# Hybrid MLA/FoX decoder layer: latent columns as seven half-block products, raw operand sums kept in DRAM

## The chip, the core and the metric

One core of a Trainium2 chip runs the whole layer in one launch. The metric is the device time of that launch in microseconds (us), the median over the runs. The engines are TensorE (PE, with its weight loads PEld), VectorE (DVE), ScalarE (ACT), GpSimd (POOL) and SyncE (SP). SP and POOL issue nearly all the DMAs here, and each has its own queue (q1 for SP, q0 for POOL).

## What is computed

One decoder layer on 512 tokens of width 2048, batch 1, all float32. One input projection gives the latents and gates of eight MLA heads and the q, k, v, forget logits and gates of eight FoX heads:

```python
h = _rms_norm(x, g_pre)
proj = h @ w_in              # 768 | 512 | 64 | 1024 | 1024 | 1024 | 1024 | 8 | 1024 columns
(q_lat, kv_lat, k_rope_raw, gate_mla, fq, fk, fv, f_logit, gate_fox) = jnp.split(proj, ...)
o_mla = _mla_branch(q_lat, kv_lat, k_rope_raw, g_q, w_uq, g_kv, w_ukv, cos, sin) * silu(gate_mla)
o_fox = _fox_branch(fq, fk, fv, f_logit, b_forget) * silu(gate_fox)
o = jnp.concatenate([o_mla, o_fox], axis=-1) @ w_out
return x + _rms_norm(o, g_post)
```

In `_mla_branch` the two latents (768 and 512 columns, together the first 1280 of `w_in`) are normalised over their own width before `w_uq` and `w_ukv` are applied; both branches are causal softmax attention.

## The kernel before

**Three matmuls for one.** A float32 operand is divided into a high part rounded to the matmul format (a cast on ACT) and a low part, the rest (a subtraction on DVE). `mm3` multiplies high x high, high x low and low x high. The normalised input stands transposed in SBUF as `hh` and `hl`, 16 tiles of 128 x 512 each.

**Weights in chunks.** All weights come in one list, `chunks`, 512 KB in most cases. `chunk(i)` starts loads up to four chunks ahead on SP (`load`, tile `raw`, three buffers) and divides up to two ahead (`divide`: `whi` on ACT, `wlo` on DVE, three buffers each). A load waits on SP until the buffer's last `wlo` is done, and everything behind it in SP's order waits too.

**Order of the stages.** FoX heads in four pairs (to 408 us), the latents (408 to 525), the products of the MLA gate group "m" (525 to 605), the four pairs of MLA heads (605 to some 760, tiles `mq`, `mk`, `mv`), the output projection (from 738 on, beside the last heads). The latents go through `proj_T`: five groups of 256 columns, 16 k-tiles, two outputs of 128 x 512, so 480 matmuls of width 512 into the tiles `l`.

**Seven products.** The gate group (2048 x 1024 weights, 512 tokens) and the two halves of the output projection are multiplied in Strassen's manner. Weights and activations are each cut into 2 x 2 blocks, and seven block products `p1, p2, p4, q6, g5, g7, g3` replace eight. Each product is 8 k-tiles of four chunks, and accumulates in two PSUM banks. This needs sums of weight blocks and sums of activation blocks.

- *Weight sums* `t7, t5, t6, t4` are made in DRAM in the background, by DMA alone. The list `bg` has one entry for each sum; `add_step` works off one per step: on POOL the accumulation of the entry before (L287), on SP a copy of 512 KB from DRAM to DRAM (L290), and for the next entry a *mark* (L292), a tiny DMA whose source is the current `whi`, so that the next copy waits until PE's work has come that far. Each call of `behind` counts a k-tile in `state["tiles"]`; when the count reaches `state["pace"]`, it is set to 0 and a step is made.
- *Activation sums* `g5, q6, g3, g7` are made on DVE, divided at once into high and low parts (`operand_steps`), and for the gate group and the first two k-pairs of the output projection stored to DRAM by POOL as 512 KB of two parts (`put_away`) and fetched by SP before use (`fetch`).

**Work beside the matmuls.** `todo` holds small steps; `pump` takes some after each k-tile, `drain` all. `latent` squares a latent and multiplies it by its gain; `latent_scale` makes the normalising factor, spreads it to a row with two matmuls (`make_row`) and scales; `part_latents` divides the ten scaled latents into `qn` and `kn` during the gate products. A scheduler sets the final order on each engine, and each engine works strictly in that order.

Of the kernel before, what the change touches and what calls it, by code (L numbers as in the profile page):

```python
# [12 lines left out]
F32 = mybir.dt.float32  # L13
# [3 lines left out]
ALU = mybir.AluOpType  # L17
AX = mybir.AxisListType

P = 128  # L20
# [43 lines left out]
def tile_hybrid_layer(  # L64
# [181 lines left out]
    state = {"loaded": 0, "divided": 0, "tiles": 0, "turn": 0, "step": -1, "pace": 7}  # L246
# [29 lines left out]
    lat = [add_chunks(w_in, [(0, 256 * p, 256)], NK, 4, 256) for p in range(5)]  # L276
# [42 lines left out]
    def gate_block(j, h, c):  # L319
        k = 2 * j + 8 * h  # L320
        return w_in[0, k * P : (k + 2) * P, O_GM + 512 * c : O_GM + 512 * (c + 1)].rearrange("(k p) c -> p k c", p=P)

    sum_blocks("m", gate_block)
    add_products(
        [(n, "m") for n in ("p1", "p4", "p2", "q6", "g5", "g7", "g3")],
        lambda g, h, c: add_chunks(w_in, [(0, O_GM + 512 * c, 512)], 8, 2, 512, 8 * h),
# [134 lines left out]
    def behind(w):  # L461

        if state["step"] <= len(bg):
            state["tiles"] += 1
            if state["tiles"] >= state["pace"]:
                state["tiles"] = 0
                add_step(state["step"], w[0:1, 0, 0:16].bitcast(F32))
                state["step"] += 1
        if done:
            state["turn"] += 1  # L470
            if later and state["turn"] % 3 == 0:
                later.popleft()()
# [329 lines left out]
    def operand_steps(of, j, pair, names, raw_of, place, then=None):  # L802

        a = {}
        raw = {}

        def block(n):
            if not a:
                for h in range(2):
                    for t in range(2):  # L810
                        a[f"a{t + 1}{h + 1}"] = pair[h][:, :, t * HALF : (t + 1) * HALF]
            return raw[n] if n in raw else a[n]

        def make(n, x, y):
            raw[n] = raw_of(f"r{of}{n}{j}").rearrange("p (h c) -> p h c", h=2)
            dve.tensor_tensor(out=raw[n], in0=block(x), in1=block(y), op=ALU.subtract)

        def part(n):
            both = place(f"s{of}{n}{j}").rearrange("p x (h c) -> p x h c", h=2)
            split_into(both[:, 0], both[:, 1], block(n))  # L820
            oper.setdefault((n, of), [None] * 4)[j] = both
            if then is not None:
                then(n, of, j)

        steps = []
        for n in names:
            if n == "sums":
                steps += [
                    lambda: make("g5", "a21", "a22"),
                    lambda: make("q6", "a11", "g5"),  # L830
                    lambda: part("g5"),
                    lambda: part("q6"),
                    lambda: make("g3", "a12", "q6"),
                    lambda: part("g3"),
                    lambda: make("g7", "a21", "a11"),
                    lambda: part("g7"),
                ]
            else:
                steps.append(lambda n=n: part(n))
        return steps  # L840
# [4 lines left out]
    def head_steps(j, names, raw_of, place, then=None):  # L845

        return operand_steps("o", j, (o_of[K1[j]], o_of[K2[j]]), names, raw_of, place, then)
# [3 lines left out]
    def put_away(n, of, j):  # L851

        away[n, of, j] = dr.tile([P, 1024], F32, name=f"away{of}{n}{j}")
        pool.dma_start(
            away[n, of, j].rearrange("p (x h c) -> p x h c", x=2, h=2), oper[n, of][j].bitcast(F32)
        )

    def fetch(n, of, j):
        both = slot(f"b{of}{n}{j}", F32R)
        nc.sync.dma_start(both.bitcast(F32), away[n, of, j].rearrange("p (x c) -> p x c", x=2))  # L860
        oper[n, of][j] = both.rearrange("p x (h c) -> p x h c", h=2)
# [10 lines left out]
    def product(name, g, parts, o, first, last, rate=1, at=None, held=0, side=()):  # L872
# [5 lines left out]
        def step(j, kk, t, hi, lo):  # L878
            mm3(
                o[t], *parts(kk, t), hi[:, j, :], lo[:, j, :], first and kk == 0, last and kk == 7,  # L880
                skip_group_check=True,
            )

        rng = list(prods[name, g])
        for i in rng[: len(rng) - held]:
            hi, lo = chunk(i)
            for j in range(2):
                if at is not None and kk == at[0]:
                    at[1]()
                for t in range(2):  # L890
                    step(j, kk, t, hi, lo)
                kk += 1
                pump(rate)
                if side and not held and kk % 2 == 0:
                    side.popleft()()
# [9 lines left out]
    def x_steps(j):  # L905
# [10 lines left out]
        later.extendleft(reversed(operand_steps("m", j, pair, ("sums",), tmp, part_slot, put_away)))  # L916
# [132 lines left out]
    for j in (1, 0):  # L1049
        todo.append(  # L1050
            lambda j=j: todo.extendleft(
                reversed(head_steps(j, ("a11", "a12", "a22", "sums"), tmp, part_slot, put_away))
            )
        )
# [11 lines left out]
    raw = []  # L1066
    state["pace"] = 6
    LAT = (("q", 0, 6, QR), ("k", 6, 10, KVR))
# [4 lines left out]
    def latent(i, o, to):  # L1073

        j = int(i >= LAT[1][1])
        acc, first = accs[:, j, :], i == LAT[j][1]
        dst = acc if first else tmp(f"lq{i}")
        act.square(dst, o)
        act.mul(to, o, gcol[:, NK + i : NK + i + 1])
        if not first:  # L1080
            dve.tensor_tensor(out=acc, in0=acc, in1=dst, op=ALU.add)
        raw.append(to)

    def latent_scale(j):

        name, lo, hi, width = LAT[j]
# [14 lines left out]
        dg = diagonals(y, f"lr{name}")  # L1101

        def scale(i):
            dve.tensor_tensor(out=raw[i], in0=raw[i], in1=acc, op=ALU.mult)


        nothing = [lambda: None] * 4
        todo.extendleft(
            reversed([*nothing, *nothing[:2], lambda: make_row(acc, f"lr{name}", *dg), *nothing, *(lambda i=i: scale(i) for i in range(lo, hi))])
        )  # L1110

    for p in range(5):
        lb = [proj_bank(f"l{p}{i}") for i in range(2)]
        proj_T(lat[p], [(lb[i], P, two[i]) for i in range(2)], hh, hl)
        both = slot(f"lat{p}")
        for i in range(2):
            latent(2 * p + i, lb[i], both[:, i, :])
        if p == 2:
            wait(6)
            todo.append(lambda: latent_scale(0))  # L1120
            wait(4)
            todo.append(rotary_key)

    gm = []
    qn, kn = [], []

    def part_latents():

        for to, name, ts in ((qn, "qn", raw[:6]), (kn, "kn", raw[6:])):
            for i, t in enumerate(ts):  # L1130
                todo.append(lambda to=to, i=i, t=t, name=name: to.append(split(t, f"{name}{i}")))
# [7 lines left out]


# [27 lines left out]

    wait(8)
    todo.append(lambda: latent_scale(1))  # L1170
    A, B = ([proj_bank(f"g{n}{t}") for t in range(2)] for n in "ab")
    product("p1", "m", x_block(0, 0), A, True, True, side=fetches("q6", "m"))
    pa, pb = slot("gpa"), slot("gpb")
    scaled_copy(pa, A, 0)
    scaled_copy(pb, A, 2)
    product("p4", "m", x_block(1, 2), B, True, True, side=fetches("g5", "m")[:2])
    c21 = slot("gc21")
    scaled(c21, B, 2, pb)
    product("p2", "m", x_block(1, 0), A, False, True, side=fetches("g5", "m")[2:])
    c11 = slot("gc11")  # L1180
    scaled_copy(c11, A, 0)
    C = [proj_bank(f"gc{t}") for t in range(2)]
    product("q6", "m", operand("q6", "m"), C, True, True, side=fetches("g7", "m"))
    c12 = slot("gc12")
    scaled(c12, C, 0, pa, ALU.subtract)
    G = [proj_bank(f"gd{t}") for t in range(2)]
    product("g5", "m", operand("g5", "m"), G, True, True, side=fetches("g3", "m"))
    c22 = slot("gc22")
    scaled(c22, G, 2, pb, ALU.subtract)
    part_latents()  # L1190
# [5 lines left out]
    product("g3", "m", operand("g3", "m"), G, False, True, 2)  # L1196
# [4 lines left out]
    state["pace"] = 7  # L1201
# [3 lines left out]
    qnh, qnl = zip(*qn)  # L1205
    knh, knl = zip(*kn)


    for p in range(4):
        c = mla[p]  # L1210
        qb = [proj_bank(f"mq{p}{i}") for i in range(3)]
# [155 lines left out]
    assert state["step"] > len(bg) and not later  # L1367
# [16 lines left out]
    product("p1", 1, operand("a11", "o"), A2, True, True, side=[*fetches("q6", "o"), lambda: load_gp(0)])  # L1384
# [9 lines left out]
    product("p2", 0, operand("a12", "o"), A, False, True, 2, (6, heads_end))  # L1394
    inner.close()
# [9 lines left out]
    product("p4", 0, operand("a22", "o"), B, True, True, 2)  # L1405
# [8 lines left out]
    def three(g, C, G, f):  # L1414

        product("q6", g, operand("q6", "o"), C, True, True, side=[] if g else [*fetches("g7", "o"), lambda: load_gp(1)])
        v = og_of[0, 2 * g + 1] = slot(f"c12{g}")
        sub(v, C, p1[g])
        product("g5", g, operand("g5", "o"), G, True, True, side=[] if g else fetches("g3", "o"))
        e = og_of[1, 2 * g + 1] = slot(f"c22{g}")  # L1420
        sub(e, G, p1[g])
        product("g7", g, operand("g7", "o"), C, False, True, side=[] if g else [lambda: load_gp(2), lambda: load_gp(3)])
# [63 lines left out]
```

## Time and profile before

| | |
|---|---|
| median of 3 runs | 913.91 us (911.92 to 914.56) |
| the profiled execution | 913.89 us, its span 912.0 us |
| granted TensorE clock | 0.997 |
| busy: PE, DVE, ACT, POOL | 902.1, 597.4, 413.7, 77.1 us |
| DMA | 196.21 MB, mean 215 GB/s; q1 (SP) 152.03 MB, q0 (POOL) 43.00 MB |

The rows quoted further down come from four views. A row of a stretch has its start and end, its length, the busy time of each engine with its count of instructions, the granted clock, the DMA share and GB/s. A row of a timeline has start, length, engine, line, operation and the tiles written and read; consecutive instructions of one kind are merged and counted, and an idle time ahead of them stands in square brackets at the end. A DMA row has a queue, its packets, MB and its share of the 16 DMA engines. Matmuls are pipelined, so their lengths overlap and only the distance of their starts tells the throughput.

### The profile page before, as it was taken

To read this page: it belongs to the slowest core of one execution; us is meant where nothing else is said; L and a number is where in the kernel's file an instruction comes from. 1 tells how busy PE (TensorE), PEld (TensorE's weight loads), DVE (VectorE), ACT (ScalarE), POOL (GpSimd) and SP (SyncE) were. 2 spreads that over 40 slices of the span, in tenths; PEclk is the share of its full clock that TensorE was granted. 3 is DMA by queue.
4 is the path that set the end of the run, shared out by engine and by line. 5 is a ranking of instruction groups with operands and counts; after the bars stand their busy time and mean duration, and the time that the engine had idled before them with its cause. 6 is when DMAs were issued, how large, how long until landed. Compare 5 with 4: busy or idle time off the path is not lost.

```text
span 912.0 us, 12251 instructions
## 1 busy us (share of the span) xinstructions
PE 902.1 (99%) x4444; PEld 765.9 (84%) x4444; DVE 597.4 (66%) x1042; ACT 413.7 (45%) x771; POOL 77.1 (8%) x101
## 2 busy tenths in 40 slices
PE   8999999999999999999999999999999999999997
PEld 7988888898889988888888888888888888888885
DVE  3467779437466674673554556777978895876686
ACT  4773333234223442342434354644454465644474
POOL 1001101010111110111221100000000000000021
PEclk9999999999999999999999999999999999999999
DMA  9367876886877988887899998877322146787868
GB/s 290 92 177 188 233 192 172 220 188 182 210 218 221 259 188 229 251 242 192 253 336 310 259 319 297 301 240 179 92 84 75 47 140 223 242 319 229 276 189 254
DMA packets 119809, 196.21 MB, mean 215 GB/s; under 512 B 15650, under 2 KB 67388, under 8 KB 119748
## 3 DMA queue, kind: packets, MB, share of 16 engines
q1 hardware_dynamic: 103556, 152.03, 51.8%
q0 software_dynamic: 15456, 43.00, 22.6%
q8 instruction: 35, 0.57, 0.3%
q10 hardware_dynamic: 736, 0.40, 0.2%
q14 instruction: 26, 0.21, 0.1%
HBM read 175.45 MB, written 70.27 MB: 269 GB/s over the span
## 4 chain that ended last, share of the span: by engine, by line
PE 94%; DMA 3%; DVE 1%; ACT 1%; issue 0%; SPq 0%; ACTq 0%
PE fv L535 5%; PE l L138 4%; PE l L140 4%; PE l L139 4%; PE fg L138 3%; PE fq L140 3%; PE fq L138 3%; PE fq L139 3%; PE fg L140 3%; PE fg L139 3%; PE fk L139 3%; PE fk L140 3%; PE fk L138 3%; PE sm L578 3%; PE fv L140 2%; PE fv L138 2%
## 5 line engine op out<-in xcount | busy, mean ns | idle before, releaser
L243 DVE TENSOR_TENSOR wlo<-raw,whi 128x1024 fp32r<-128x1024 f32 (+3 forms) x193 | 228.1, 1184 | 175.5 <-ACT whi L242 168.0
L242 ACT CAST whi<-raw 128x1024 fp32r<-128x1024 f32 (+3 forms) x193 | 196.7, 1021 | 269.4 <-PE fk L139 48.7
L138 PE MATMUL l<-h,whi 128*128 128x512 f32 x160 | 63.3, 396 | 0.0
L140 PE MATMUL l<-h,wlo 128*128 128x512 f32 x160 | 62.4, 390 | 0.0
L139 PE MATMUL l<-h,whi 128*128 128x512 f32 x160 | 62.4, 390 | 0.0
L138 PE MATMUL fq<-h,whi 128*128 128x512 f32 x128 | 52.6, 411 | 0.0
L138 PE MATMUL fg<-h,whi 128*128 128x512 f32 x128 | 51.0, 398 | 0.0
L140 PE MATMUL fq<-h,wlo 128*128 128x512 f32 x128 | 50.3, 393 | 0.0
L140 PE MATMUL fg<-h,wlo 128*128 128x512 f32 x128 | 50.1, 392 | 0.0
L139 PE MATMUL fq<-h,whi 128*128 128x512 f32 x128 | 50.1, 391 | 0.0
L138 PE MATMUL fk<-h,whi 128*128 128x512 f32 x128 | 50.0, 391 | 0.0
L139 PE MATMUL fg<-h,whi 128*128 128x512 f32 x128 | 49.9, 390 | 0.0
L139 PE MATMUL fk<-h,whi 128*128 128x512 f32 x128 | 49.8, 389 | 0.0
L140 PE MATMUL fk<-h,wlo 128*128 128x512 f32 x128 | 49.8, 389 | 0.0
L140 PE MATMUL fv<-whi,h 128*128 128x256 f32 (+1 forms) x128 | 39.5, 309 | 0.0
L139 PE MATMUL fv<-wlo,h 128*128 128x256 f32 (+1 forms) x128 | 39.5, 309 | 0.0
L138 PE MATMUL fv<-whi,h 128*128 128x256 f32 (+1 forms) x128 | 39.5, 309 | 0.0
L535 PE MATMUL fv<-whi,h 128*128 128x456 f32 x128 | 39.2, 392 | 0.0
L140 PEld LDWEIGHTS l<-h,wlo 128*128 128x128 f32 x160 | 30.0, 188 | 6.4
L287 POOL DMA_DIRECT2D t<-in_w_out_dram x16 | 18.7, 1168 | 198.0 <-DMA t<-in_w_out_dram 197.6
L138 PEld LDWEIGHTS l<-h,whi 128*128 128x128 f32 x160 | 30.1, 188 | 6.0
L139 PEld LDWEIGHTS l<-h,whi 128*128 128x128 f32 x160 | 30.1, 188 | 5.7
(484 smaller groups left out, 2210.3 us busy)
## 6 DMA issues: line engine op xcount, KB each, us to landing
raw<-in_w_in_dram SPq DMA_DIRECT2D x84, 512.0 KB
t<-in_w_out_dram SPq DMA_DIRECT2D x32, 512.0 KB
raw<-t SPq DMA_DIRECT2D x32, 512.0 KB
raw<-in_w_out_dram SPq DMA_DIRECT2D x24, 512.0 KB
t<-in_w_out_dram POOLq DMA_DIRECT2D x16, 512.0 KB, 8.3
t<-t POOLq DMA_DIRECT2D x16, 512.0 KB, 8.2
awaymg<-smg POOLq DMA_DIRECT2D x12, 512.0 KB, 6.8
bmg<-awaymg SPq DMA_DIRECT2D x12, 512.0 KB
```

The lines of the kernel that those rows point to most:

```text
L138: pe.matmul(o, ah, bh, start=first, stop=False, **kw)
L139: pe.matmul(o, ah, bl, start=False, stop=False, **kw)
L140: pe.matmul(o, al, bh, start=False, stop=last, **kw)
L242: act.copy(hi[:, :m], raw[:, :m])
L243: dve.tensor_tensor(out=lo[:, :m], in0=raw[:, :m], in1=hi[:, :m].bitcast(F32), op=ALU.subtract)
L287: pool.dma_start(to.rearrange("p (k c) -> p k c", k=2), second, accum_op=ALU.add)
L535: pe.matmul(banks[t][:, :n], a[k][:, tss[t]], b[:, j, :], start=k == 0 and m == 0, stop=k == NK - 1 and m == 2,)
L578: pe.matmul(s[:, :nn], a[:, qs], c[:, :nn], start=(i == 0), stop=(i == len(pairs) - 1))
```

## The change

- The first 1024 latent columns are computed as seven products (group "l"), in turn with those of the gate group. They are `turned`: the weights are the stationary operand, so the result comes out with the latent columns on the partitions, 128 x 256 per block; the activation operands are those of the gate group and are shared. Only the last 256 columns still go through `proj_T`. `lat_sum` and `lat_less` combine the blocks.
- The sums of the latent weights join `bg` (64 entries instead of 48).
- Activation operands go to DRAM as raw fp32 sums (256 KB each) and are divided after the fetch (`part_fetched`).
- The steps of `bg` are counted in `paced`, which `product` calls too; the count is lowered by the pace. The pace is 6, then 4, then 1000 from product p1 of the latents on, 6 from product g5 of the gate group on, 2.5 in the MLA heads, 4 in the output projection.
- A latent is scaled and divided in one step (`latent_part`), ten of them in `todo` from product q6 of the gate group on.

```diff
-            if state["tiles"] >= state["pace"]:
-                state["tiles"] = 0
+            if state["tiles"] >= state["pace"]:
+                state["tiles"] -= state["pace"]
...
-    lat = [add_chunks(w_in, [(0, 256 * p, 256)], NK, 4, 256) for p in range(5)]
+    lat = add_chunks(w_in, [(0, 1024, 256)], NK, 4, 256)
...
+    for g in "lm":
+        sum_blocks(g, lambda j, h, c, g=g: in_block(g, j, h, c))
     add_products(
-        [(n, "m") for n in ("p1", "p4", "p2", "q6", "g5", "g7", "g3")],
+        [
+            *((n, g) for n in ("p1", "p2", "p4") for g in "lm"),
+            *((n, g) for g in "lm" for n in ("q6", "g5", "g7", "g3")),
+        ],
...
     def fetch(n, of, j):
         both = slot(f"b{of}{n}{j}", F32R)
-        nc.sync.dma_start(both.bitcast(F32), away[n, of, j].rearrange("p (x c) -> p x c", x=2))
-        oper[n, of][j] = both.rearrange("p x (h c) -> p x h c", h=2)
+        nc.sync.dma_start(both[:, 1, :].bitcast(F32), away[n, of, j])
+        oper.setdefault((n, of), [None] * 4)[j] = both.rearrange("p x (h c) -> p x h c", h=2)
+
+    def part_fetched(n, of, j):
+        both = oper[n, of][j]
+        split_into(both[:, 0], both[:, 1], both[:, 1].bitcast(F32))
...
+            for f in range(2):
+                c = slice((2 * t + f) * P, (2 * t + f + 1) * P)
+                mm3(
+                    o[t][:, f * HALF : (f + 1) * HALF], hi[:, j, c], lo[:, j, c], *parts(kk),
+                    first and kk == 0 and f == 0, last and kk == 7, skip_group_check=True,
+                )
...
                 pump(rate)
+                paced(hi)
...
+    def latent_part(i):
+        j = int(i >= 6)
+        dve.scalar_tensor_tensor(
+            out=raw(i), in0=raw(i), scalar=gcol[:, NK + i : NK + i + 1], in1=accs[:, j, :],
+            op0=ALU.mult, op1=ALU.mult,
         )
+        latents[i] = split(raw(i), f"ln{i}")
...
+    state["pace"] = 1000
...
+    product("q6", "l", sums_wide("q6"), C, True, True, side=along(divisions("g5", "m"), fetches("g7", "m")), turned=True)
...
+    for i in range(10):
+        todo.append(lambda i=i: latent_part(i))
...
+    state["pace"] = 6
+    product("g5", "m", operand("g5", "m"), G, True, True)
...
-    state["pace"] = 7
+    state["pace"] = 2.5
```

How the order on the engines moves, at two places. In what follows g5/0 is the first of the four chunks of the gate group's product g5, g3/1 the second of product g3.

SP, from the last chunks of product g7 to the plain chunks of product g3 (read from `w_in`), before:

```order
L221 DMA raw_5110<-t7m_107 128x1024
L860 DMA bmg_5128<-awaymg_3232 128x1024
L221 DMA raw_5130<-t7m_108 128x1024
L860 DMA bmg_5148<-awaymg_3588 128x1024
L230 DMA raw_5153<-in_w_in_dram 128x2x512
L230 DMA raw_5177<-in_w_in_dram 128x2x512
L230 DMA raw_5201<-in_w_in_dram 128x2x512
L230 DMA raw_5225<-in_w_in_dram 128x2x512
```

and at the same place now (`t_...` are sums of output weights, `whi_5365` and so on the chunk whose high half a mark waits for):

```order
L221 DMA raw_5411<-t7m_124 128x1024
L290 DMA t_152<-in_w_out_dram 128x2x512
L290 DMA t_144<-in_w_out_dram 128x2x512
L292 DMA t_148<-whi_5365 1x16
L292 DMA t_153<-whi_5365 1x16
L230 DMA raw_5446<-in_w_in_dram 128x2x512
L290 DMA t_148<-in_w_out_dram 128x2x512
L290 DMA t_153<-in_w_out_dram 128x2x512
L292 DMA t_165<-whi_5389 1x16
L292 DMA t_157<-whi_5389 1x16
L230 DMA raw_5470<-in_w_in_dram 128x2x512
L290 DMA t_165<-in_w_out_dram 128x2x512
```

Between two chunk loads there now stand two copies and two marks, where there was nothing or an operand fetch.

DVE, from a chunk of product g7 to one of product g3, before (`qn`, `kn` are low halves of latents, `wlo` those of chunks):

```order
L243 TENSOR_TENSOR wlo_5204<-raw_5153,whi_5203 128x1024
L243 TENSOR_TENSOR wlo_5228<-raw_5177,whi_5227 128x1024
L130 TENSOR_TENSOR kn_5237<-lat_4531,kn_5237 128x512
L130 TENSOR_TENSOR kn_5246<-lat_4531,kn_5246 128x512
L130 TENSOR_TENSOR kn_5264<-lat_4683,kn_5264 128x512
L243 TENSOR_TENSOR wlo_5255<-raw_5201,whi_5254 128x1024
```

and now, from the low half of chunk g7/1 to that of g7/3 (L1165 scales a latent, `ln` is its low half):

```order
L243 TENSOR_TENSOR wlo_5414<-raw_5363,whi_5413 128x1024
L130 TENSOR_TENSOR ln_5511<-lat_4344,ln_5511 128x512
L130 TENSOR_TENSOR ln_5524<-lat_4345,ln_5524 128x512
L1165 SCALAR_TENSOR_TENSOR lat_4345<-lat_4345,gcol,ls 128x512
L1165 SCALAR_TENSOR_TENSOR lat_4780<-lat_4780,gcol,ls 128x512 x2
L130 TENSOR_TENSOR ln_5543<-lat_4345,ln_5543 128x512
L130 TENSOR_TENSOR ln_5556<-lat_4780,ln_5556 128x512
L243 TENSOR_TENSOR wlo_5449<-raw_5387,whi_5448 128x1024
L130 TENSOR_TENSOR ln_5578<-lat_4780,ln_5578 128x512
L1165 SCALAR_TENSOR_TENSOR lat_4781<-lat_4781,gcol,ls 128x512 x2
L1165 SCALAR_TENSOR_TENSOR lat_3743<-lat_3743,gcol,ls 128x512
L130 TENSOR_TENSOR ln_5591<-lat_4781,ln_5591 128x512
```

Seven latent operations now stand between two chunks' low halves, where up to four stood before.

225 lines of the change are left out of this document (145 added, 80 removed).

## The prediction, made before the changed kernel ran

> **What bounds the kernel now.** I read the busy times on the page first, then the stretches of the projection stages.
>
> ```profile
> PE 902.1 (99%) x4444; PEld 765.9 (84%) x4444; DVE 597.4 (66%) x1042; ACT 413.7 (45%) x771; POOL 77.1 (8%) x101
> 410.00:526.00 116.00, 116.00 (x532) 96.15 (x531) 57.30 (x84) 44.44 (x70) 20.72 (x27) 1.00 0.96 268
> 526.00:608.00 82.00, 81.71 (x375) 67.60 (x374) 56.26 (x75) 44.31 (x59) 0.00 (x0) 1.00 0.84 288
> 608.00:740.00 132.00, 131.97 (x752) 114.74 (x751) 107.23 (x216) 66.45 (x161) 2.81 (x3) 1.00 0.39 110
> ```
>
> TensorE (PE) is the bound: 902.1 of 912.0 us, and it hardly stops in the latent stage (410 to 526), the gate products (526 to 608) or the MLA heads (608 to 740). So its time is the number of matmuls times their spacing, plus any stop that the change makes. The durations on the page overlap; the spacing is read from start times. In the timeline of PE these two rows of width 512 stand 84 matmuls apart, and the two of width 256 stand 42 apart:
>
> ```profile
> 254.92 0.39 PE L140 MATMUL fk<-h,wlo 128*128 128x512 f32 x1
> 273.96 0.39 PE L140 MATMUL fk<-h,wlo 128*128 128x512 f32 x1
> ...
> 175.88 0.28 PE L138 MATMUL fv<-whi,h 128*128 128x256 f32 x1
> 180.92 0.28 PE L138 MATMUL fv<-whi,h 128*128 128x256 f32 x1
> ```
>
> 19.04/84 = 0.2267 us at width 512, and 5.04/42 = 0.1200 us at width 256. Half the width costs 53% of the time.
>
> The third thing to see is how little room the gate products leave. Their chunk holds 12 matmuls of width 512, so PE eats one in 2.72 us. VectorE (DVE) near their end:
>
> ```profile
> 584.04 1.40 DVE L1148 SCALAR_TENSOR_TENSOR gc<-gd,hcol,gpb 128x512 f32<-128x512 f32 x2
> 585.36 1.28 DVE L130 TENSOR_TENSOR qn<-lat,qn 128x512 fp32r<-128x512 f32 x2
> 586.56 1.22 DVE L243 TENSOR_TENSOR wlo<-raw,whi 128x1024 fp32r<-128x1024 f32 x1
> 587.69 2.49 DVE L130 TENSOR_TENSOR qn<-lat,qn 128x512 fp32r<-128x512 f32 x4
> 590.10 2.35 DVE L243 TENSOR_TENSOR wlo<-raw,whi 128x1024 fp32r<-128x1024 f32 x2
> 592.37 1.89 DVE L130 TENSOR_TENSOR kn<-lat,kn 128x512 fp32r<-128x512 f32 x3
> 594.18 1.22 DVE L243 TENSOR_TENSOR wlo<-raw,whi 128x1024 fp32r<-128x1024 f32 x1
> 595.32 0.68 DVE L130 TENSOR_TENSOR kn<-lat,kn 128x512 fp32r<-128x512 f32 x1
> 595.92 1.40 DVE L1148 SCALAR_TENSOR_TENSOR gc<-gc,ncol,gc 128x512 f32<-128x512 f32 x2
> 597.24 1.40 DVE L1148 SCALAR_TENSOR_TENSOR gc<-gc,hcol,gc 128x512 f32<-128x512 f32 x2
> 598.55 1.21 DVE L243 TENSOR_TENSOR wlo<-raw,whi 128x1024 fp32r<-128x1024 f32 x1
> ```
>
> No row has an idle time behind it: DVE is full from 584 on, and PE loses only the 0.3 us of the stretch above. Back to back, a low half of a latent costs 0.62 us (2.49/4), a scaled sum 0.70, a chunk's low half 1.18.
>
> **The matmuls.** Of the 480 latent matmuls of width 512, 96 stay and 384 go; seven products of 8 k-tiles, 4 blocks and 3 terms add 672 of width 256. 384 x 0.2267 = 87.0 us less, 672 x 0.1200 = 80.6 us more: **-6.4 us**, all on the path, as nothing else on PE changes in number. This sign holds as long as a matmul of width 256 takes under 0.1295 us.
>
> The Trainium skill ("TensorE: Matmul & The Clock Gate", Back-to-back issue gap) gives N/2.4 + 2.5 ns when warm, 215.8 and 109.2 ns here, by which it would be -9.5 us. The trace does not agree (226.7 and 120.0 ns, both some 11 ns longer).
>
> **Seven products instead of proj_T: chunks.** 28 chunks of 512 KB replace 16: 12 more loads, casts and low halves. PE takes 24 x 0.1200 = 2.88 us per latent chunk and 2.72 per gate chunk. The gate products of before live on the same diet (288 GB/s, PE short by 0.3 us), with 512 KB operand fetches between; the fetches now halve. DVE gets 1.18 for the chunk, 0.62 for an operand division, and 1.4 of sums per product: 8.6 of 11.5 us. Bank reads lie behind the product of the other group that runs between. I take 0 us here; up to 3 if a fetch delays a load.
>
> **Raw sums put away, divided on return.** As many divisions as before (30 operands), later. Those of the gate group fall into the latent products (above); four fall into the first MLA heads, where DVE has 25 of 132 us free; the other ten, of 0.62 us, fall into the output products. Half the bytes go out and back. 0 us, up to 2 in the output products.
>
> **The latents' end.** Before, ten scalings ran early, and only the ten low halves stood in the full stretch. Now scaling and low half stand together, at about 0.65 + 0.62 us each, with two row copies and four scaled sums, between the low halves of chunks g7/1 and g3/0. They can't start sooner: the first row copy needs a matmul that stands 42 matmuls into product g5. Let t be counted from the start of product g5. DVE gets the rows at 11 and is through chunk g7/1 at 17, where PE wants it at 14.9. The next two chunks have 7 latent operations each ahead of them: 7 x 0.63 + 1.18 = 5.6 us against 2.72, twice 2.9 us late. Then g3/0 stands behind the scaled sums, which need the end of g7 (4 x 0.70 + 1.18, 4 us), and g3/1 behind four gate operations (3 us). Together **about 15 us**, between 12 and 17.
>
> **The block sums' debt.** Setting the pace to 1000 doesn't drop the count: `tiles` goes on rising through eleven products, to about 88, and is now lowered by the pace and no longer set to 0. At pace 6 each further call fires a step: two per chunk, 18 from g5/0 to g3/0. So SyncE (SP) gets, between two chunk loads, two DRAM copies of 512 KB and two marks, and the copies wait until the marks of the round before have landed. Four marks (L292) with what follows, in the latent stage of before, in SP's timeline:
>
> ```profile
> 423.59 0.24 SPq L292 DMA_DIRECT2D t<-whi  x1
> 424.85 0.37 SPq L230 DMA_DIRECT2D raw<-in_w_in_dram  x1
> 425.27 0.56 SPq L290 DMA_DIRECT2D t<-in_w_out_dram  x1
> ...
> 443.28 0.24 SPq L292 DMA_DIRECT2D t<-whi  x1
> 444.73 0.37 SPq L230 DMA_DIRECT2D raw<-in_w_in_dram  x1
> 448.16 0.56 SPq L290 DMA_DIRECT2D t<-in_w_out_dram  x1
> 455.80 0.24 SPq L292 DMA_DIRECT2D t<-whi  x1
> 457.06 0.37 SPq L230 DMA_DIRECT2D raw<-in_w_in_dram  x1
> 459.85 0.56 SPq L290 DMA_DIRECT2D t<-in_w_out_dram  x1
> 460.51 0.57 SPq L230 DMA_DIRECT2D raw<-in_w_in_dram  x1
> 461.29 0.34 SPq L292 DMA_DIRECT2D t<-whi  x1
> 463.10 0.37 SPq L230 DMA_DIRECT2D raw<-in_w_in_dram  x1
> 467.36 0.60 SPq L290 DMA_DIRECT2D t<-in_w_out_dram  x1
> ```
>
> A mark keeps SP for 1.26 us (455.80 to 457.06), a copy for 0.66 (459.85 to 460.51), and from mark to copy it takes 1.7, 4.9, 4.1 and 6.1 us; the 1.7 with an idle queue ahead of the mark. A round is then that wait, two copies and the first mark: wait + 2.6 us. I take 4.1 (the two longer ones shared the DMA with stores that run elsewhere now): 6.7 us. The ends are 4.3 and 8.7; I lean to the upper rows, because now two copies always stand ahead of the marks.
>
> Copies 3 and 4 issue at about t = 9, as they stand behind the load into the buffer that chunk g5/3 frees. The second chunk of query weights has its last part behind copy 17: seven rounds later, 9 + 7 x 6.7 = 56. It lands some 4.5 us on and takes 1.9 to divide: 62.4. Without stops PE would want it after three products of 10.9 us, 0.9 us of matmuls for the rows, and 18 matmuls of the first query chunk: 32.6 + 0.9 + 4.1 = 37.6. So PE is **24.8 us** late (8 to 39 for the two ends). DVE's 15 us lie inside it: both hold PE at the same chunks, and the later one counts, so that 15 is the least. Behind this chunk the debt is nearly paid and the heads have DMA to spare (0.39 of it busy before).
>
> **The sum.** The profiled execution took 913.89 us (span 912.0 plus 1.9), the median of the runs is 913.91: no correction. 913.9 - 6.4 + 24.8 = **932.3 us**.
>
> **Rivals.**
> *VectorE alone.* If rounds take under 5.3 us (waits under 2.7), the queue keeps ahead of DVE and the 15 us decide: 913.9 - 6.4 + 15 = 922.5 (919.5 to 924.5). For it: the mark that took 1.7 us, and copies that are no longer mixed with stores. Against it: no mark with a transfer fresh ahead of it took under 4.1. 20%.
>
> *The DMA engines saturate.* For it, two neighbouring stretches of 8 us, without and then with accumulations running, queue by queue, and the latent stage as a whole:
>
> ```profile
> q1 hardware_dynamic: 875, 3.20, 100.2%
> ...
> q0 software_dynamic: 397, 1.02, 83.4%
> q1 hardware_dynamic: 148, 0.45, 17.8%
> ...
> DMA packets 17345, 31.12 MB, mean 268 GB/s; under 512 B 968, under 2 KB 8648, under 8 KB 17338
> ```
>
> SP's queue (q1) moved 3.20 MB in 528:536 and 0.45 MB in 520:528, while the accumulations of POOL's queue (q0) had 83% of the engines. Up to the second query chunk stand 17 copies, 10 loads and about 15 accumulations, 42 x 0.524 = 22 MB. At 268 GB/s that is 82 us, from t = -3 to 79; with the division 81, so 43 us late: 950. Against it: an accumulation waits for its copy, so POOL can't keep its queue full. 12%. The Trainium skill ("DMA: Bandwidth & Descriptors", Queues, rings and completion order) has each engine turn between its queues packet by packet, which speaks for this case; the two stretches agree in kind.
>
> *Faster after all.* The lead hides everything: three raw buffers and chunks divided two ahead give PE about 8 us of stock, so it runs dry only where rounds stay above 2.72 us for long, and only if DVE's rows between the low halves of g7/0 and g3/0, 23 us by the durations above, fit into four chunks' 10.9. Then 913.9 - 6.4 = 907.5. DVE's own rows speak against it. 9%. A stop that just eats the 6.4 us leaves no change: 2%.
>
> **Numbers.** The forecast has 57%. I call 0.3% (2.7 us) the least that a measurement of this kernel tells from no change. Faster 0.09, same 0.02, slower 0.89. The range takes in the DVE case and the longer rounds up to 8.7 us (913.9 - 6.4 + 39 = 946.5): 918 to 947, leaving out the fast case and most of the saturated one.
>
> **What would show it.** Right: latent products at 0.120 us per matmul with PE full until product g5; PE idle of 20 to 30 us between g5 and the second query chunk; SP rounds of two L290 and two L292 some 6 to 7 us apart; casts waiting on raw. DVE full from g5's end to g3/0. Wrong: PE full through g7 and g3 (faster), or stops in the latent products themselves, or a spacing at width 256 over 0.13 us.

## The result, and the profile after

The changed kernel takes 964.89 us (median of 4 runs, 962.62 to 968.46); the kernel before took 913.03 on the same chip. The ratio is 1.057 (1.0531 to 1.061): 52 us slower, where 932.3 us, at most 947, had been forecast. The profiled execution took 962.62 us, its span 960.8.

Where the time went is read from the starts of the stages. The timeline of PE before, at the first matmul of the latents, of the gate group's product g5, of the first MLA heads and of the output projection:

```profile
408.78 0.39 PE L138 MATMUL l<-h,whi 128*128 128x512 f32 x1
...
570.20 0.39 PE L138 MATMUL gd<-whi,bmg 128*128 128x512 f32 x1
...
605.20 0.39 PE L138 MATMUL mq<-qn,whi 128*128 128x512 f32 x1
...
737.96 0.48 PE L138 MATMUL oa<-whi,boa 128*128 128x512 f32 x1
```

and the same four after:

```profile
406.22 0.39 PE L138 MATMUL l<-h,whi 128*128 128x512 f32 x1
...
560.14 0.48 PE L138 MATMUL gdm<-whi,bmg 128*128 128x512 f32 x1
...
631.54 0.39 PE L138 MATMUL mq<-ln,whi 128*128 128x512 f32 x1
...
786.18 0.48 PE L138 MATMUL oa<-whi,boa 128*128 128x512 f32 x1
```

From latents to g5 the new kernel is 7.5 us quicker (153.9 against 161.4); from g5 to the heads it loses 36.4 (71.4 against 35.0), from there to the output projection 21.9 (154.6 against 132.8), and behind it 0.6. With the 2.6 us of the start that is the 48.8 us by which the spans differ. The stretches of the kernel after (start and end, length, busy time of PE, PEld, DVE, ACT and POOL, granted clock, DMA share, GB/s):

```profile
406.00:560.00 154.00, 154.00 (x1019) 141.57 (x1017) 98.08 (x114) 76.50 (x98) 5.72 (x8) 1.00 0.76 230
...
575.00:632.00 57.00, 33.72 (x102) 23.09 (x100) 25.63 (x35) 16.89 (x22) 11.07 (x11) 0.73 1.01 246
632.00:690.00 58.00, 42.87 (x198) 34.64 (x198) 28.09 (x46) 18.83 (x37) 8.79 (x9) 0.88 1.06 259
```

PE is full from the latents to product g5, and from 575 on stands still for 23.3 and 15.1 us in two stretches in which the DMA engines are busy throughout and VectorE less than half of the time. What PE waits for between 575 and 690 us (us in total, times, longest), and what ScalarE's casts wait for there:

```profile
PE gcm L138 <- ACT whi L242: 11.3, 3, 7.4
PE mq L138 <- ACT whi L242: 8.4, 1, 8.4
PE gdm L138 <- ACT whi L242: 8.3, 2, 7.2
...
ACT whi L242 <- DMA t<-whi: 24.4, 9, 7.1
```

Of the seven casts of chunks from 575 to 625 us none waits last for its own load. Six wait for marks (`t<-whi`) and one for PE: a mark reads the high half of an earlier chunk, and there are three such buffers, so the next cast into that buffer has to wait until the mark has landed. Only from 630 on, with the query weights (`in_w_uq`), does a cast wait for a load (19.0 us in three waits). The chain of work that ended last runs through the same marks (start and time from issue to landing, in us):

```profile
576.98 5.10 DMA t<-whi
...
583.57 11.13 DMA t<-whi
...
596.17 5.06 DMA t<-whi
...
602.75 12.66 DMA t<-whi
```

SP's next copies wait for the same marks, and the loads stand in SP's order behind the copies. SP's timeline after:

```profile
565.94 1.85 SPq L290 DMA_DIRECT2D t<-in_w_out_dram  x2
...
575.71 1.22 SPq L290 DMA_DIRECT2D t<-in_w_out_dram  x2
...
582.10 1.42 SPq L290 DMA_DIRECT2D t<-in_w_out_dram  x2
...
584.70 0.40 SPq L230 DMA_DIRECT2D raw<-in_w_in_dram  x1
594.72 1.41 SPq L290 DMA_DIRECT2D t<-in_w_out_dram  x2
...
601.25 1.46 SPq L290 DMA_DIRECT2D t<-in_w_out_dram  x2
...
615.42 1.22 SPq L290 DMA_DIRECT2D t<-in_w_out_dram  x2
...
636.24 0.56 SPq L290 DMA_DIRECT2D t<-in_w_out_dram  x1
```

The rounds have the forecast's form, but between 575.71 and 615.42 four of them take 39.7 us: 9.9 us each, not 6.7, alternately short (6.4 and 6.5) and long (12.6 and 14.2). The marks take 34 of the 39.7 us, 8.5 each, where the prediction had 4.1. The queues between 590 and 610 us, with packets, MB and share of the 16 engines:

```profile
q1 hardware_dynamic: 1747, 3.36, 56.2%
q0 software_dynamic: 608, 1.67, 46.3%
```

The engines are full, and POOL's accumulations (q0) hold 46% of them for a third of the bytes. (Such a share is the time that the packets took; whether they spend it in the engines or waiting for the memory behind them, no run here separates.) Per 512 KB (0.524 MB) that is 1.75 us on q1 and 2.91 us for an accumulation. A round of two copies, a load and two accumulations then costs 3 x 1.75 + 2 x 2.91 = 11.1 us of engine time.

### The profile page after: what moved, and what is told of

Read it like the earlier page. It is cut to its first block, busy times and chain, and to the rows that moved or that the text cites. A ratio compares the mean times of both kernels' runs of the same rounds, so it can differ in the third digit from the quotient of the medians.

```text
span 960.8 us, 12945 instructions
## 1 busy us (share of the span) xinstructions
PE 912.9 (95%) x4732; PEld 781.3 (81%) x4732; DVE 619.3 (64%) x1066; ACT 424.4 (44%) x779; POOL 87.5 (9%) x105
## 4 chain that ended last, share of the span: by engine, by line
PE 84%; DMA 12%; DVE 2%; SPq 1%; ACT 1%; issue 0%; ACTq 0%; DVEq 0%
DMA t<-whi 5%; PE fv L545 4%; DMA raw<-in_w_uq_dram 4%; PE fg L138 3%; PE fq L140 3%; PE fq L138 3%; PE fq L139 3%; PE fg L140 3%; PE fg L139 3%; PE fk L139 3%; PE fk L140 3%; PE fk L138 3%; PE sm L588 2%; PE fv L140 2%; PE fv L139 2%; PE fv L138 2%
## 5 line engine op out<-in xcount | busy, mean ns | idle before, releaser
L243 DVE TENSOR_TENSOR wlo<-raw,whi 128x1024 fp32r<-128x1024 f32 (+3 forms) x205 | 242.9, 1186 | 223.8 <-ACT whi L242 213.6
L242 ACT CAST whi<-raw 128x1024 fp32r<-128x1024 f32 (+3 forms) x205 | 209.4, 1022 | 337.2 <-PE fk L139 48.5
L138 PE MATMUL mq<-ln,whi 128*128 128x512 f32 x72 | 30.6, 425 | 10.3 <-ACT whi L242 8.4
L139 PE MATMUL mq<-ln,whi 128*128 128x512 f32 x72 | 29.6, 411 | 0.0
L140 PE MATMUL mq<-ln,wlo 128*128 128x512 f32 x72 | 29.5, 413 | 0.0
L1409 POOL DMA_DIRECT2D c<-in_x_dram x8 | 7.1, 963 | 238.9 <-ACT c L1408 238.7
L605 ACT ACTIVATE pf<-sf,stf 128x128 f32<-128x128 f32 (+3 forms) x32 | 16.9, 528 | 26.9 <-DVE stf L603 26.9
L140 PEld LDWEIGHTS fq<-h,wlo 128*128 128x128 f32 x128 | 24.0, 188 | 5.4
```

What stands on the lines that cost most here:

```text
L138: pe.matmul(o, ah, bh, start=first, stop=False, **kw)
L139: pe.matmul(o, ah, bl, start=False, stop=False, **kw)
L140: pe.matmul(o, al, bh, start=False, stop=last, **kw)
L242: act.copy(hi[:, :m], raw[:, :m])
L243: dve.tensor_tensor(out=lo[:, :m], in0=raw[:, :m], in1=hi[:, :m].bitcast(F32), op=ALU.subtract)
L605: act.activation(p, s[:, :n], AF.Exp, bias=st[:, 0:1], accum_out=st[:, 1:2])
```

## Experiments

Times are compared as ratios with the kernel before, run on the same chip in turn (911.4 to 912.3 us there).

**1. The kernel after without the debt.**

```diff
     state["pace"] = 6
+    state["tiles"] = 0
     product("g5", "m", operand("g5", "m"), G, True, True)
```

> The count is set to 0 where the pace returns to 6, so the 18 overdue steps are not fired between g5/0 and g3/0; four steps fall into products g5, g7 and g3, the rest into the MLA heads. Theory debt: all of the loss that came from the steps goes (41.1 us of PE stops and 13.6 us of matmuls at a lowered clock in the profile after), and only VectorE's end is left: 913.0 - 6.4 + 15 = 921.6 us, between 918 and 926. Rival VectorE: the scaling and low halves of the latents hold PE for much more than 15 us by themselves, so the time stays above 940. Rival hidden: VectorE holds nothing once the loads come in time, 906.6 us.

Measured: 913.92 us, ratio 1.0023 (1.0008 to 1.0038). One line gives back all but some 2 us of the loss, and more than was expected of it. The stretches of its profile:

```profile
575.00:600.00 25.00, 22.37 (x107) 18.25 (x106) 23.65 (x33) 15.37 (x22) 2.38 (x3) 1.00 0.93 257
600.00:640.00 40.00, 36.60 (x188) 30.47 (x187) 27.26 (x46) 18.84 (x37) 4.78 (x6) 0.96 0.92 231
```

PE stops for 2.6 + 3.4 = 6.0 us in place of 38.4. So the debt is the cause, and VectorE's end costs far less than the 15 us put down for it. What is left are three stops of the gates (3.4, 1.6 and 1.1 us between 575 and 660 us); none waits for a chunk's low half, which is what the 15 us were counted at. VectorE's timeline in this run:

```profile
585.23 1.22 DVE L243 TENSOR_TENSOR wlo<-raw,whi 128x1024 fp32r<-128x1024 f32 x1
586.36 2.07 DVE L1165 SCALAR_TENSOR_TENSOR lat<-lat,gcol,ls 128x512 f32<-128x512 f32 x3
588.35 1.28 DVE L130 TENSOR_TENSOR ln<-lat,ln 128x512 fp32r<-128x512 f32 x2
589.55 1.22 DVE L243 TENSOR_TENSOR wlo<-raw,whi 128x1024 fp32r<-128x1024 f32 x1
```

At most five latent operations stand here between two low halves of chunks, where the order shown ahead of the prediction had seven, and the low halves stand 2.3 to 4.3 us apart, where the prediction had 5.6. In the kernel after VectorE was not even full there. It had time to wait 7 us for a late chunk:

```profile
596.06 1.23 DVE L243 TENSOR_TENSOR wlo<-raw,whi 128x1024 fp32r<-128x1024 f32 x1 [6.99 <-ACT whi L242]
```

The code of the latents is the same in both. The scheduler's order changed when the steps went.

**2. The debt without its accumulations.**

```diff
-        if n > 0:
+        if n > 0 and not state.get("bare"):
             to, _, second = bg[n - 1]
             pool.dma_start(..., accum_op=ALU.add)
...
     state["pace"] = 6
+    state["bare"] = True
```

> The overdue steps stay, but from product g5 on no accumulation is issued on POOL's queue (the later sums of output weights lack their second block). Theory bytes: a round of two copies, two accumulations and a chunk load moves 2.62 MB at 253 GB/s, 10.4 us; without the accumulations 1.57 MB, 6.2 us. By the prediction's own sum the second query chunk is then 9 + 7 x 6.2 + 6.4 - 37.6 = 21 us late instead of 50, and the lowered clock takes some 7 us: 913.0 - 6.4 + 21 + 7 = 935 us, between 925 and 945. Rival marks: the round is the time that a mark takes behind the copies in SP's own queue, and POOL's accumulations run beside it: unchanged within 1%, 955 to 966 us.

Measured: 925.93 us, ratio 1.0146 (1.0112 to 1.018), at the low end of what the theory of bytes gave, and 30 us from the rival. The accumulations on POOL's queue, whose sums PE does not need before the output projection, carry about three quarters of the loss: 5.7% falls to 1.5%. The marks still stand in SP's queue, but they land sooner: from 574.87 to 597.87 us four rounds take 23.0 us, 5.75 each, no copy waits longer than 3.8 us for a mark, and the casts wait 3.7 us for marks in all. The edit also takes away the later accumulations, in the heads, which the kernel before has too; so the burst's own part may be somewhat less.

**3. The debt without marks.**

```diff
-        if n + 1 < len(bg):
+        if n + 1 < len(bg) and not state.get("bare"):
             nc.sync.dma_start(bg[n + 1][0][0:1, 0:16], mark)
```

> The overdue steps stay with copies and accumulations, but from product g5 on no mark is issued, so no copy on SP waits for a mark to land. Theory bytes: the same 2.62 MB per round pass through the same engines, so PE waits as long: 955 to 966 us. Rival marks: a round is only the issue of two copies and a load, some 2 us, the queue keeps ahead of PE, and VectorE's 15 us decide: 922 us, up to 930.

Measured: 968.32 us, ratio 1.0614 (1.0593 to 1.0636). The number fits the theory, but the run can't speak for it: without its mark nothing ties a copy to its place, and the scheduler put the copies of the output weights at the head of the program, where PE stopped instead: SP's timeline has four of these copies in a row at 17.09 us. A stretch behind them:

```profile
20.00:160.00 140.00, 100.96 (x395) 79.97 (x394) 51.31 (x88) 45.93 (x108) 26.34 (x27) 0.85 1.05 266
```

39 us of stops at a DMA share of 1.05, in another place. The question of the marks was put again in run 4.

**4. The marks on ScalarE's queue.**

```diff
-            nc.sync.dma_start(bg[n + 1][0][0:1, 0:16], mark)
+            (act if state.get("apart") else nc.sync).dma_start(bg[n + 1][0][0:1, 0:16], mark)
...
     state["pace"] = 6
+    state["apart"] = True
```

> The debt is kept with all its copies and accumulations, in their places; only the marks from product g5 on are issued by ScalarE on its own queue, so that a mark no longer stands behind two copies of 512 KB in SP's queue. Theory bytes: the engines move the same 2.62 MB per round, so the time stays within 1%: 956 to 970 us. Rival marks: a mark with an empty queue ahead of it took 1.7 us, a round is then 4.3 us, and by the prediction's sum PE is late by no more than VectorE's part: 914 to 931 us.

Measured: 959.38 us, ratio 1.0517 (1.0492 to 1.0542). What SP's copies wait for between 575 and 690 us (total, times, longest), in the kernel after and then in this run:

```profile
SPq L290 <- DMA t<-whi: 52.0, 8, 10.7
```

```profile
SPq L290 <- DMA t<-whi: 8.3, 2, 7.0
```

SP's waits for marks are nearly gone, and yet its chunk loads (at 584.63, 594.76 and 603.23 us) keep their rhythm, 9.3 us apart. ScalarE's casts in the same stretch now wait for those loads:

```profile
ACT whi L242 <- DMA raw<-in_w_in_dram: 18.2, 3, 7.1
```

PE gains 5 us of 52. The wait for the mark was mostly the form in which SP and the casts felt full engines, not their cause: with the marks out of the way the loads themselves come late. The marks are not quite gone as a cause, since in ScalarE's own order they hold one cast back for 8.6 us, so 5 us may be a little less than they cost.

**5. Plain copies for accumulations.**

```diff
-            pool.dma_start(..., second, accum_op=ALU.add)
+            how = {} if state.get("plain") else {"accum_op": ALU.add}
+            pool.dma_start(..., second, **how)
...
     state["pace"] = 6
+    state["plain"] = True
```

> The debt is kept, with every transfer in its place and on its queue; only the accumulations from product g5 on are made plain copies of the same 512 KB (the later sums of output weights then hold the second block alone). In the profile after, between 590 and 610 us, q1 had 56.2% of the engines for 3.36 MB and q0 46.3% for 1.67 MB: 1.75 us per copied and 2.91 us per accumulated 512 KB. Theory: an accumulated byte costs the engines 1.66 times a copied one, so a round of five transfers falls from 11.1 to 8.8 us, the stops by about a fifth: 948 to 957 us. Rival: only the count of bytes matters: unchanged, 960 to 968 us.

Measured: 947.54 us, ratio 1.0381 (1.0346 to 1.0417): a third of the loss goes though every byte that the profile counts is still moved. POOL's queue between 590 and 610 us:

```profile
q0 software_dynamic: 659, 2.40, 33.1%
```

512 KB on q0 now take 33.1% x 20 / 2.40 x 0.524 = 1.45 us of the engines, half of the 2.91 of an accumulation.

**6. The debt on the kernel before.**

```diff
-    state["pace"] = 6
+    state["pace"] = 1000
...
+                if state.get("due", 0) and state["step"] <= len(bg):
+                    state["due"] -= 1
+                    add_step(state["step"], hi[0:1, 0, 0:16].bitcast(F32))
+                    state["step"] += 1
...
+    state["due"] = 18
     product("g5", "m", operand("g5", "m"), G, True, True, side=fetches("g3", "m"))
```

> The kernel before with its own latents and operands, only its steps withheld from the latent stage on and 18 of them fired from the gate group's product g5 on, one per k-tile. Theory debt: the burst by itself costs what it cost in the kernel after, about 41 us of stops and 14 us of lowered clock, less what operand fetches of 512 KB no longer compete for: 945 to 967 us. Rival: the burst hurts only together with the new end of the latents on VectorE: below 925 us.

Measured: 971.06 us, ratio 1.0644 (1.0625 to 1.0663), a little over the range. The old kernel with the old latents loses as much by the burst alone, and its casts wait 40.0 us for marks between 570 and 690 us:

```profile
570.00:640.00 70.00, 42.91 (x143) 30.54 (x142) 24.55 (x31) 18.64 (x25) 11.13 (x11) 0.78 1.02 276
```

**7. Matmuls in the stops.** The granted clock of 0.73 and 0.88 in the stretches after was no part of the prediction. Behind a stop the matmuls follow at 0.43 us instead of 0.227; PE's timeline after:

```profile
596.08 1.22 PE L138 MATMUL gcm<-whi,bmg 128*128 128x512 f32 x2 [7.36 <-ACT whi L242]
...
597.93 0.63 PE L140 MATMUL gcm<-whi,bmg 128*128 128x512 f32 x1
598.36 0.63 PE L139 MATMUL gcm<-wlo,bmg 128*128 128x512 f32 x1
```

Taken over both stretches, 33.7 us of busy time at 0.73 and 42.9 at 0.88 would lose 33.7 x 0.27 + 42.9 x 0.12 = 14 us, by estimate. Is that a loss of its own?

```diff
+    FILL = {("g7", "m", 2): 7, ("g7", "m", 4): 12, ("g7", "m", 6): 32, ("g3", "m", 2): 31, ("g3", "m", 4): 6}
+    def fill(n, hi):
+        if n:
+            to = bank("pv", "fill", 1)
+        for _ in range(n):
+            pe.matmul(to, hi[:, 0, :P], hi[:, 1, :], start=True, stop=True, skip_group_check=True)
...
+            fill(FILL.get((name, g, kk), 0), hi)
```

> The kernel after, with 7, 12, 32, 31 and 6 matmuls of width 512 more, whose results nobody reads, ahead of the five chunks of products g7 and g3 that PE waits for most: 88 x 0.2267 = 19.9 us of work laid into the stops, so that PE doesn't pause there. Theory clock: the slow matmuls behind these stops (1.5, 2.4, 1.6, 2.3 and 2.0 us in the profile after) run at full clock, and the time falls by 5 to 9 us, to 956 to 960. Rival engines: the chunks land when the DMA engines let them, and a faster matmul only waits longer for the next one: unchanged, 962 to 967 us.

Measured: 966.82 us, ratio 1.0595 (1.0573 to 1.0616), as after.

```profile
575.00:632.00 57.00, 44.75 (x174) 34.02 (x173) 22.08 (x29) 12.52 (x16) 11.07 (x11) 0.94 1.03 250
```

The clock in the products rises from 0.73 to 0.94 (the added matmuls counted in), and the products end no earlier: their last matmul starts at 631.72 us, in the kernel after at 631.31. While transfers decide when a chunk is there, a quick matmul only waits longer for the next. For the heads the run says nothing: the order there changed, and PE now stops 7.9 us for gates.

**8. Without the debt, with earlier row copies.**

```diff
     state["pace"] = 6
+    state["tiles"] = 0
...
-    wait(6)
+    wait(10)
...
-    product("q6", "m", operand("q6", "m"), C, True, True)
+    product("q6", "m", operand("q6", "m"), C, True, True, 2)
```

> No overdue steps (as in the first run of this call), and VectorE's end begins about 7 us earlier: product q6 of the gate group takes two steps of the list per k-tile, with ten empty steps in place of six ahead of the row copies. Theory: with the debt gone VectorE is the last cause, and its end now has four more k-tiles to spread over: 8 to 15 us less than the run without debt, 907 to 914 us. Rival: what is left without the debt isn't VectorE's: the same time as that run within 2 us.

Measured: 912.46 us, ratio 1.0003 (0.9991 to 1.0016), 0.2% under run 1, far less than the 8 us that VectorE's rows were thought to give. What was left were stops of the gates; the longest, 2.7 us, was the second query matmuls' wait for a scaled sum that frees their bank.

**9. GpSimd scales the latents, and no step runs in the gate products.**

```diff
-        if i >= 8:
-            act.copy(raw(i), o)
+        act.mul(raw(i), o, gcol[:, NK + i : NK + i + 1])
...
-        dve.scalar_tensor_tensor(
-            out=raw(i), in0=raw(i), scalar=gcol[:, NK + i : NK + i + 1], in1=accs[:, j, :],
-            op0=ALU.mult, op1=ALU.mult,
-        )
+        pool.tensor_tensor(out=raw(i), in0=raw(i), in1=accs[:, j, :], op=ALU.mult)
...
-    state["pace"] = 6
...
-    state["pace"] = 2.5
+    state["pace"], state["tiles"] = 2, 0
```

> No step of the block sums runs in the gate products at all (the 23 that are left run in the MLA heads, one per two k-tiles), a latent is multiplied by its gain on ScalarE when it is squared, and by its row on GpSimd (1.28 us by the only row of such an operation), so VectorE has ten operations of 0.69 us less in products g5 to g3. Theory: without the debt the last stops (6.2 us, and 2.3 us of lowered clock, at 593 to 610 us in the run without debt) are VectorE's, and go: the time before less 6.4 us, up to 2 us more, so 905 to 908 us where the kernel before takes 911.4. Rival: those stops are the gates' own chain (scaled sum, transposition, tanh, product), which only moves: 912 to 914 us.

Measured: 920.74 us, ratio 1.0096 (1.0068 to 1.0124). Both theories missed it. GpSimd's and VectorE's groups:

```profile
L1164 POOL TENSOR_TENSOR lat<-lat,ls 128x512 f32<-128x512 f32 x10 | 17.2, 1756 | 121.2 <-DVE ls L449 121.2
```

```profile
L130 DVE TENSOR_TENSOR ln<-lat,ln 128x512 fp32r<-128x512 f32 x8 | 11.6, 1497 | 0.0
...
L1213 DVE SCALAR_TENSOR_TENSOR gc<-gdm,hcol,gpb 128x512 f32<-128x512 f32 x2 | 1.4, 739 | 0.0
```

Beside GpSimd's work a low half of a latent takes 1.50 us on VectorE, against 0.68 in run 1 (mean of the group between 571 and 592 us in both). What VectorE was to be spared it lost on its own operations. The edit changes two things at once: run 12 below has the same pace of steps without GpSimd's scaling, and its ratio is 1.0036, so part of the 1.0096 is likely the steps'.

**10 to 12. Three trims of run 8.** Run 10 issues the scaled sum at once; run 11 also puts all gates behind product g3; run 12 is run 10 with no steps in the gate products (as in run 9).

```diff
-    todo.append(lambda: scaled(c12, G, 0, c12))
+    scaled(c12, G, 0, c12)
```

> As the run without debt and with early rows, and the scaled sum that frees the bank of product g3 is issued right behind the product, not put at the end of the list: it stood behind a chunk's low half, and PE waited 2.7 us at the second query matmuls for the bank. Theory: that stop goes, 909 to 911 us where the kernel before takes 911.4. Rival: the low half of the chunk is late in its place: the same as that run, 912 to 913 us.

Measured: 911.69 us, ratio 0.9985 (0.997 to 1.0), between the two. The stop of 2.7 us is gone, and one of 2.4 us for a gate stands in the first heads instead.

```diff
-    for f in range(4):
-        todo.append(lambda f=f: gate(f, c11, c21))
...
-    for f in range(4, 8):
-        todo.append(lambda f=f: gate(f, c12, c22))
+    for f in range(8):
+        todo.append(lambda f=f: gate(f, *((c11, c21) if f < 4 else (c12, c22))))
```

> As the run before it in this call, and the four gates of the upper half are put behind product g3 too, so that no transposition stands in products g7 and g3 waiting for VectorE's scaled sums (stops of 1.3 and 0.9 us). Theory: another 1 to 2 us less, 907 to 910 us. Rival: the gates then meet the first MLA heads' own work on VectorE, and PE stops there instead: 911 to 915 us.

Measured: 913.04 us, ratio 1.0001 (0.9985 to 1.0018): the rival's side.

```diff
-    state["pace"] = 6
-    state["tiles"] = 0
     product("g5", "m", operand("g5", "m"), G, True, True)
...
-    state["pace"] = 2.5
+    state["pace"], state["tiles"] = 2, 0
```

> As the second run of this call, and the four steps of the block sums in products g5 to g3 are moved into the MLA heads too (one per two k-tiles there). Theory: the chunk loads meet no accumulation in the products, 1 to 2 us less than the second run. Rival: with more steps in the heads their weight loads are late instead, as in the run in which GpSimd scaled the latents: 1 to 4 us more.

Measured: 916.26 us, ratio 1.0036 (1.0016 to 1.0056), the rival again, a little over its 1 to 4 us. With the steps away PE is full in the products (560 to 600 us; VectorE, busy for 39.7 of the 40 us, holds nothing up), and stands still for 4 us from 600 to 640 and 3 us from 640 to 737, in the heads, instead.

Run 10 is the best found; its gain of 0.15% is under the 0.3% that can be told from no change. By the starts of its stages, against the kernel before, it is 7.4 us quicker from latents to g5 (154.0), 1.6 slower in the gate products (36.6, 0.9 of it the row matmuls) and 5.1 slower in the heads (137.9 against 132.8). So the gain of the matmuls is spent mostly in the heads.

## Why the prediction was wrong, point by point

- **The matmuls, -6.4 us: right.** The 7.5 us from latents to g5 hold 0.9 us of row matmuls that now stand behind g5's start; 6.6 remain. In the timeline after, two matmuls of width 256, 28 apart:

```profile
501.53 0.28 PE L139 MATMUL gcl<-bmq,whi 128*128 128x256 f32 x1
...
504.89 0.28 PE L140 MATMUL gcl<-bmq,wlo 128*128 128x256 f32 x1
```

  3.36/28 = 0.1200 us, as taken.
- **Chunks, raw sums and divisions at nothing: right.** PE is full in all 154 us of the products with group "l", and the output projection changed by 0.6 us. The 2.6 us at the start are no effect of these: runs 1 and 8 carry the same code there and begin the latents at 405.81 and 407.76 us.
- **The place of the loss: right; its form: half right.** The debt stops PE from product g7 on; run 1 takes it away and run 6 makes it alone. But the prediction had the loads late behind the copies, with "casts waiting on raw" as its sign. In the products the casts wait for marks instead, which hold the buffers of the high halves; only at the second query chunk, where the sum was made, is it a load behind a copy.
- **The size of a round, 6.7 us: wrong, and the step that failed.** The wait from mark to copy, 4.1 us, was read off the latent stage, with one copy and one accumulation to a mark, and carried over as if it were a latency. It measured 8.5 us on the average, because it is mostly the time the DMA engines need for what is queued: a round took 9.9 us, 11.1 by engine time. The forecast's seven rounds, from copies 3 and 4 (565.94) to copy 17 (636.24), took 70.3 us in place of 46.9. With them the prediction's own path reads 5.8 + 70.3 + 9.5 = 85.6 us after the start of g5, where it had 9 + 46.9 + 6.4 = 62.3: the whole miss at this chunk is in the rounds, give or take 3 us at either end. Run 2 agrees with the rest of the sum: with its rounds of 5.75 us the sum gives 913.9 - 6.4 + (9 + 7 x 5.75 + 6.4 - 37.6) = 925.6, and 925.9 were measured (927 by the ratio); that the two agree so closely is partly luck, as the sum counts no loss behind this chunk. The argument against the saturated rival, "an accumulation waits for its copy, so POOL can't keep its queue full", fell: q0 had 45.5% of the engines over the whole 72 us from g5 to the heads:

```profile
q0 software_dynamic: 2248, 5.82, 45.5%
```

- **The saturated rival, 12%: right in kind, and at its place in size.** It had PE 43 us late at the second query chunk. PE gets there at 645.8, t = 85.6, against 37.6 without stops: 48. With 27 plain transfers at 1.75 and 15 accumulations at 2.91 its sum is 91 us of engine time where it had 82.
- **"Behind this chunk the debt is nearly paid": wrong.** Accumulations and late head weights filled the engines to 690 us, at a share of 1.06 from 632 on. PE's stop ahead of the second query chunk, 8.4 us, is part of the 21.9 us lost between heads and output projection; the rest, some 13 us, came after it, and neither forecast nor rival had it.
- **VectorE's 15 us as a floor: wrong.** Run 1 stops for 6.0 us, all of it for gates. Seven latent operations per chunk were counted in an order that the scheduler had made with the late loads in it, and were taken for a property of the code.
- **The range's top, 947,** followed from rounds of 8.7 us and left the saturated case outside. It should have reached past it, for q0's 83% of the engines in the rows of before was direct evidence.

What stays open is why run 6 loses 0.7% more than the kernel after with the same count of overdue steps, why the rounds are alternately short and long, and what exactly costs run 10 its 5 us in the heads. None was tried further.

## What to carry to other kernels

Cost background transfers in engine time per queue, and sum it over the stretch: a wait that a transfer shows in the trace may be mostly the work queued ahead of it, as here, and then won't hold when that work is doubled. A tiny transfer that reads a buffer holds the buffer until it has landed, so a mark between full queues can stop the engine that fills the buffer. A counter that goes on counting while its consumer is off becomes a burst at the moment the consumer returns; look at what a pace does on re-entry before looking at anything else. An order printed by a scheduler belongs to the whole program, and another edit can dissolve the crowding that one reads in it.

## What the runs showed of the hardware

- **An accumulating DMA costs the engines twice a plain one.** 512 KB from DRAM to DRAM on POOL's queue: 2.91 us of the 16 engines as an accumulation (kernel after), 1.45 as a copy (run 5), both with the engines nearly full. In the rows of before from 520 to 528 us it was more: 83.4% x 8 / 1.02 x 0.524 = 3.4 us.
- **Behind short stops the clock sometimes falls.** In the timeline after, pauses of 1.13 and 0.53 us, two matmuls apart, are followed by 0.43 us per matmul:

```profile
623.53 0.73 PE L138 MATMUL gdm<-whi,bmg 128*128 128x512 f32 x2 [1.13 <-ACT whi L242]
624.79 0.50 PE L139 MATMUL gdm<-wlo,bmg 128*128 128x512 f32 x1 [0.53 <-DVE wlo L243]
...
625.77 0.63 PE L140 MATMUL gdm<-whi,bmg 128*128 128x512 f32 x1
626.20 0.63 PE L138 MATMUL gdm<-whi,bmg 128*128 128x512 f32 x1
```

  Two pauses of the same form, no shorter, are not; here 0.24 us per matmul follow:

```profile
577.05 0.73 PE L138 MATMUL gcm<-whi,bmg 128*128 128x512 f32 x2 [1.41 <-ACT whi L242]
578.31 0.50 PE L139 MATMUL gcm<-wlo,bmg 128*128 128x512 f32 x1 [0.53 <-DVE wlo L243]
...
578.89 0.40 PE L139 MATMUL gcm<-wlo,bmg 128*128 128x512 f32 x1
579.13 0.40 PE L140 MATMUL gcm<-whi,bmg 128*128 128x512 f32 x1
```

  So the length of the pauses alone does not decide. The first pair came some 7 us behind a stop of 7.2 us and a run of slow matmuls, the second behind full work; whether that is the reason, no run shows. The Trainium skill ("TensorE: Matmul & The Clock Gate", HAM oscillation) warns of pauses over some 3.4 us. The trace agrees that the pace halves behind longer pauses (7.36 us in run 7's rows), and shows that shorter ones can be followed by it too.
- **GpSimd's arithmetic slows VectorE's with two SBUF inputs.** 0.68 to 1.50 us for a low half, and 1.28 to 1.76 on GpSimd's own side, while the scaled sum, which reads one input from PSUM, keeps its 0.74 (run 9). The Trainium skill ("SBUF — State Buffer", SBUF: two separate sides) describes a port pair that the two engines take in turn for a whole instruction, VectorE for operations with two SBUF inputs, among others; the numbers agree.
